# Weight splits moved from POOL to DVE, matmul operands aligned, and a regrouped top-k end, in a two-block kernel on one Trainium2 core

## The chip, the cores and the metric

The kernel runs on one core of one Trainium2 chip. A core has five engines that run side by side and wait for each other by semaphores: PE (TensorE, the matrix multiplier), DVE (VectorE), ACT (ScalarE), POOL (GpSimd) and SP (SyncE, which here only starts DMA transfers). On PE the profile also tells apart PEld, the loading of weights. The metric is the device time of one execution, in microseconds (us).

## The reference

The input is x, 256 tokens of 1,024 values, in fp32. The first block:

```python
proj = h @ w_in[l]                      # h = rmsnorm(x)
attn_out = windowed_gqa(q_a, k_a, v_a, attn_sink[l])
lru_out = bidir_rglru(centred_depthwise_conv(x_l, ...), ...) * gelu(gate_l)
mem_out = memory_cross_attention(q_m, k_m, v_m)
merged = (g[:, :, 0] * (attn_out @ p_attn[l]) + g[:, :, 1] * (lru_out @ p_lru[l])
          + g[:, :, 2] * (mem_out @ p_mem[l]))
x = x + merged @ w_out[l]
x = x + peer_ffn(rmsnorm(x, g_ffn[l]), w_peer_q[l], peer_sub_keys[l], peer_u[l], peer_v[l])
```

Its feed-forward picks experts by product keys:

```python
q = (h @ w_q).reshape(b, s, PEER_HEADS, 2, PEER_HALF)       # 8 heads, 2 halves of 128
sc = jnp.einsum('bshpc,hpkc->bshpk', q, sub_keys)           # 128 keys a half
top_v, top_i = lax.top_k(sc, PEER_TOPK)                     # 16 of each half
best_v, best_pos = lax.top_k(cand_v, PEER_TOPK)             # 16 of the 256 sums
gate = jax.nn.softmax(best_v, axis=-1)
act = jax.nn.gelu(jnp.einsum('chkd,cd->chk', u_tab[idx], hx))
out = jnp.einsum('chk,chkd->cd', gate * act, v_tab[idx])    # 16,384 experts in all
```

The second block has two hybrid layers. Each computes four branches from one projection (retention, a gated depthwise convolution of 31 taps, a gMLP, and sliding-window attention of 8 heads), projects and gates them, adds their sum through `w_out`, and ends with a SwiGLU feed-forward of width 2,816.

## The kernel before

**Layout and weights.** Features lie on the 128 partitions, the 256 tokens along the free axis. All weights are cut into blocks of 128 x 128, 5,416 in all, stored in HBM in the order of use. Class `Stream` brings them: SP loads 16 blocks (1 MB) into a `raw` tile (two buffers), and for every slot of 8 blocks `_slot` makes two tiles of the reduced format fp32r: ACT copies `raw` to `whi` (L88), then DVE or POOL forms `wlo = raw - whi` (L91). This pair of instructions is called a split here. `pool_share = (m, d)` tells how many of d slots go to POOL: one in two as a rule, and all of them from the second part of the top-k to the end of that phase. `on_pool`, `on_vector` and `on_scalar` remember the last such instruction of an engine, and `issue_after` places an instruction behind it.

**Matmuls.** Every block costs three matmuls of 256 columns (`mm3`, L171 to L173): `whi` by the operand's high part, `whi` by its low part, `wlo` by its high part. The operand (128 x 256, high and low) is the moving one; in some projections (`mm3a`, L177 to L179) the weights move instead. `group`, `proj_a` and `proj_b` run these over the blocks of a projection.

**Tiles of operands.** In block 1 `T8`, `T6` and `T4` are helpers that take tiles of 8, 6 and 4 rows of 256 tokens from the pool "b1"; in a hybrid layer `T4` takes them from "m{l}", where small tiles are opened ahead of them. The trace calls all of these `t`. `hh` and `hl` are the normed input in two parts, `ga` the weighted expert activations, `fh` and `fl` the operand of the feed-forward's output projection.

**Order of the work.** The program is written as a main stream of blocks with background tasks beside it. `add` registers a generator as a task; each pair of weight blocks calls `tick`, which steps every task whose count has run out, and the number it yields is the number of ticks (times `unit`) to its next step. A list scheduler then sets the final order on each engine. Slots have raised priority.

**The expert feed-forward.** The scores of all experts are computed densely. A u-block is 8 weight blocks (24 matmuls into `pu`); its gelu goes to `ha` (L759). While the top-k runs as a task (`picks`), the main stream does u-blocks by `u_while`; `early` is their number by the end of that phase. The task takes 4 head pairs times 2 token halves: `unit` computes scores `sc` (L937), top 16 of each half (`top16`, from MAX8 at L1047), the 256 sums and the picks by one-hot products `oh` (L975 to L980), and yields `TK_PACE` ticks:

```python
                    yield TK_PACE
                    if hq == 3:
                        gates(t)
                        yield 2
                        turn(t)
```

`gates` is the softmax: DVE forms `ge` (L987), ACT its exponential (L988). `turn` transposes the picks of a half on PE into `ptk` (L241). Then `build` makes the gate matrix by one-hot products on PE (`pgb`), L846 multiplies `ha` by `hb` for the u-blocks done early, four blocks an instruction, and the V loop makes `ga` (L184, L185) and adds up the output in `acc`, with the remaining u-blocks in between.

**The mixers of a hybrid layer.** The main stream projects; beside it tasks run the convolution (taps on DVE, `t<-up,hw,t`, L1121), the attention scores (L1218 to L1233) and retention (L1264, L1267). L919 adds a projection's output to x, L295 forms the next operand's low part.

Of the kernel before, what the change touches and what calls it, by code (L numbers as in the profile page):

```python
# [7 lines left out]
F32 = mybir.dt.float32  # L8
# [11 lines left out]
P = 128  # L20
S = 256
KD = 8
# [3 lines left out]
RAW_BUFS = 2  # L26
SLOT_BUFS = 3
N_HA = 96
HALF = 64
TK_PACE = 20  # L30
T_OH = 8
# [21 lines left out]
class Stream:  # L53
# [3 lines left out]
    def __init__(self, K, pool, w):  # L57
        self.K, self.pool, self.w = K, pool, w
        self.order = []
        self.ticked = 0  # L60
        self.raw = None
        self.cur = None
        self.pool_share = (1, 2)

# [63 lines left out]
class Core:  # L128
# [111 lines left out]
    def transpose(self, out, in_):  # L240
        self.nc.tensor.transpose(out, in_, self.ident)  # L241

    def scr(self, name):
        return self.tp.tile([P, S], F32, tag="scr", name=name, bufs=N_SCR)
# [165 lines left out]
    def block1(self):  # L410
        tc, nc, a, ws = self.tc, self.nc, self.a, self.ws
        with ExitStack() as st:
            p = st.enter_context(tc.tile_pool(name="b1", bufs=1))

            def T8(dt=F32R):
                return p.tile([P, KD, S], dt, tag="t8", name="t8", bufs=2)

            def T6(dt=F32, w=S):
                return p.tile([P, 6, w], dt, tag="t6", name="t6", bufs=8)

            def T4(dt=F32):
                return p.tile([P, 4, S], dt, tag="t4", name="t4", bufs=5)

# [16 lines left out]


            xl = T6(w=S + 3)
            nc.gpsimd.memset(xl[:, :, 0:2], 0.0)
            nc.gpsimd.memset(xl[:, :, S + 2:S + 3], 0.0)
# [289 lines left out]
    def peer(self):  # L734
# [4 lines left out]
        tc, nc, a, ws = self.tc, self.nc, self.a, self.ws  # L739
        with ExitStack() as st:  # L740
            p = st.enter_context(tc.tile_pool(name="pe", bufs=1))
# [29 lines left out]
            with tc.tile_pool(name="peg", bufs=1) as gp:  # L771
# [106 lines left out]
                assert ahead == NBLK  # L878
                ws.pool_share = (1, 2)
                tl = self.tp.tile([P, LAST, 2, S], F32R, tag="ld", name="tail", bufs=1)  # L880
# [42 lines left out]
    def topk(self, tp, i1, i2, gt, iot):  # L923
        nc, a, ws = self.nc, self.a, self.ws
# [87 lines left out]
        def picks():  # L1012
            with self.tc.issue_after(ws.on_pool):
                nc.gpsimd.tensor_copy(io, self.cst[:, None, C_IO:C_IO + 16].to_broadcast([P, 32, 16]))
            for hq in range(4):
                for t in range(2):
                    while hq not in qts:
                        yield 1
                    unit(hq, t, qts[hq])
                    if hq == t == 1:  # L1020
                        with self.tc.issue_after(ws.on_pool):
                            nc.gpsimd.tensor_copy(iot, self.cst[:, C_IO:C_IO + P, None].to_broadcast([P, P, 2]))
                    yield TK_PACE
                    if hq == 3:
                        gates(t)
                        yield 2
                        turn(t)
            yield 4
# [25 lines left out]
    def mixers(self, l):  # L1054
        tc, nc, a, ws = self.tc, self.nc, self.a, self.ws
        with ExitStack() as st:
            p = st.enter_context(tc.tile_pool(name=f"m{l}", bufs=1))
            par = p.tile([P, P2_COLS], F32, tag="par2", name="par2")
# [6 lines left out]
            def T4(dt=F32):  # L1065
                return p.tile([P, 4, S], dt, tag="t4", name="t4", bufs=13)

# [367 lines left out]
    def ffn(self, l):  # L1435
        tc, nc, a, ws = self.tc, self.nc, self.a, self.ws
        with ExitStack() as st:
            p = st.enter_context(tc.tile_pool(name=f"f{l}", bufs=1))
            fh = p.tile([P, FF, S], F32R, tag="fh", name="fh")
            fl = p.tile([P, FF, S], F32R, tag="fl", name="fl")  # L1440
# [168 lines left out]
```

## Time and profile before

| | |
|---|---|
| median of 3 runs | 2208.46 us (2206.96 to 2214.88) |
| profiled execution | 2205.13 us, span 2203.3 us |
| mean granted clock of TensorE | 0.971 of full speed |
| busiest engines | PE 94%, DVE 79%, ACT 53%, POOL 33% of the span |
| splits `wlo` | 430 on DVE, mean 1268 ns; 247 on POOL, mean 2501 ns |
| moved by DMA | 370.03 MB, mean 168 GB/s |

The stages in time: block 1's mixers to about 345 us, the top-k of the experts from there to about 500, the rest of the experts to about 1170, the first layer's mixers to about 1540, its feed-forward to about 1690, the second layer's mixers to about 2045, and its feed-forward to the end. A row of the trace gives a start or a group's count, a duration, the engine, the line, the operation, and "out<-in" tiles by name with shape; in square brackets stands how long the engine was idle before it and which instruction released it. PEclk is the clock granted to TensorE as a share of full speed (1.00 is 2.4 GHz, 0.50 is 1.2).

### The profile page before, as it was taken

What the parts mean: (1) busy time and instruction counts of PE and PEld (TensorE: products, weight loads), DVE (VectorE), ACT (ScalarE), POOL (GpSimd) and SP (SyncE); (2) the same over time, 40 slices, a digit from 0 to 9 for tenths busy, and PEclk for the clock granted to TensorE, in tenths of its full rate; (3) what the DMA queues carried; (4) which work ended last, traced back from release to release, by engine and by line L of the source; (5) the groups of instructions that cost most, each with busy time, mean ns of one, the idle gap of its engine ahead of it and who ended that gap; (6) DMA issues with size and microseconds to landing.
All of it is one profiled execution on the core that took longest, in us unless ns stands there. A gap on an engine that the chain in (4) does not pass through costs nothing. (4 is left out here: it accounts for less than half of the span.)

```text
span 2203.3 us, 41676 instructions
## 1 busy us (share of the span) xinstructions
PE 2067.6 (94%) x16818; PEld 2002.5 (91%) x16818; DVE 1741.0 (79%) x3117; ACT 1159.6 (53%) x1906; POOL 734.2 (33%) x361
## 2 busy tenths in 40 slices
PE   8879999959998999999998899999999889999999
PEld 7868999959998999999998778999999778999997
DVE  8837668998999888975557999976764999976772
ACT  5648654435554555545445555466555545465543
POOL 4424746830000000000003434654444434654443
PEclk9989999979999999999999999999999999999999
DMA  5343555424553444455554533454555533445554
GB/s 194 122 126 118 189 183 181 172 84 167 179 181 138 173 173 173 173 177 194 197 188 145 190 125 143 173 183 176 197 192 193 191 131 135 168 177 175 192 192 159
DMA packets 56925, 370.03 MB, mean 168 GB/s; under 512 B 6491, under 2 KB 10140, under 8 KB 13468
## 3 DMA queue, kind: packets, MB, share of 16 engines
q1 hardware_dynamic: 50256, 357.06, 45.5%
q10 hardware_dynamic: 6476, 10.31, 1.8%
q8 instruction: 131, 2.15, 0.4%
q14 instruction: 62, 0.51, 0.1%
HBM read 364.73 MB, written 2.62 MB: 167 GB/s over the span
## 5 line engine op out<-in xcount | busy, mean ns | idle before, releaser
L88 ACT ACTIVATE whi<-raw 128x1024 fp32r<-128x1024 f32 x677 | 716.5, 1060 | 731.0 <-PE acc L172 165.9
L91 POOL TENSOR_TENSOR wlo<-raw,whi 128x1024 fp32r<-128x1024 f32 x247 | 617.5, 2501 | 1324.6 <-ACT whi L88 1238.6
L91 DVE TENSOR_TENSOR wlo<-raw,whi 128x1024 fp32r<-128x1024 f32 x430 | 545.2, 1268 | 211.7 <-ACT whi L88 209.9
L171 PE MATMUL pu<-hh,whi 128*128 128x256 f32 x1024 | 291.0, 284 | 21.9 <-ACT whi L88 21.9
L173 PE MATMUL mm<-hh,wlo 128*128 128x256 f32 x1008 | 285.7, 284 | 7.3 <-DVE wlo L91 5.0
L173 PE MATMUL pu<-hh,wlo 128*128 128x256 f32 x1024 | 286.5, 280 | 0.0
L172 PE MATMUL pu<-hl,whi 128*128 128x256 f32 x1024 | 286.4, 280 | 0.0
L172 PE MATMUL mm<-hl,whi 128*128 128x256 f32 x1008 | 285.2, 283 | 0.0
L171 PE MATMUL mm<-hh,whi 128*128 128x256 f32 x1008 | 284.7, 282 | 0.0
L172 PE MATMUL acc<-ga,whi 128*128 128x256 f32 x1000 | 269.8, 279 | 5.1 <-DVE ga L185 5.1
L173 PE MATMUL acc<-ga,wlo 128*128 128x256 f32 x1000 | 269.2, 279 | 0.0
L171 PE MATMUL acc<-ga,whi 128*128 128x256 f32 x1000 | 249.3, 281 | 4.9 <-ACT ga L184 4.9
L1121 DVE SCALAR_TENSOR_TENSOR t<-up,hw,t 128x256 f32<-128x256 f32 x240 | 215.3, 901 | 3.7
L171 PEld LDWEIGHTS pu<-hh,whi 128*128 128x128 f32 x1024 | 195.3, 191 | 22.3 <-ACT whi L88 22.3
L173 PE MATMUL pg<-hh,wlo 128*128 128x256 f32 x704 | 198.9, 283 | 9.4 <-POOL wlo L91 6.3
L173 PEld LDWEIGHTS mm<-hh,wlo 128*128 128x128 f32 x1008 | 193.1, 192 | 11.2 <-DVE wlo L91 6.2
L171 PE MATMUL pg<-hh,whi 128*128 128x256 f32 x704 | 198.5, 282 | 1.2 <-ACT whi L88 1.2
L172 PE MATMUL pg<-hl,whi 128*128 128x256 f32 x704 | 197.4, 280 | 0.0
L172 PEld LDWEIGHTS mm<-hl,whi 128*128 128x128 f32 x1008 | 193.5, 192 | 2.9 <-issue 2.7
L171 PEld LDWEIGHTS mm<-hh,whi 128*128 128x128 f32 x1008 | 193.1, 192 | 1.5 <-issue 0.8
L172 PEld LDWEIGHTS pu<-hl,whi 128*128 128x128 f32 x1024 | 194.4, 190 | 0.0
L173 PEld LDWEIGHTS pu<-hh,wlo 128*128 128x128 f32 x1024 | 194.3, 190 | 0.0
(410 smaller groups left out, 5209.5 us busy)
## 6 DMA issues: line engine op xcount, KB each, us to landing
raw<-in_w SPq DMA_DIRECT2D x336, 1024.0 KB, 4.8
raw<-in_w SPq DMA_DIRECT2D x5, 512.0 KB, 5.5
bias<-bias_scr ACTq DMA_DIRECT2D x4, 512.0 KB, 6.8
bias_scr<-sbb ACTq DMA_DIRECT2D x4, 384.0 KB
cl<-in_cstl ACTq DMA_DIRECT2D x2, 576.0 KB, 3.7
x<-in_xT SPq DMA_DIRECT2D x4, 256.0 KB, 6.5
memt<-in_memT ACTq DMA_DIRECT2D x1, 1024.0 KB, 4.9
keys<-in_keysT ACTq DMA_DIRECT2D x1, 1024.0 KB
```

The costliest lines, as they stand in the source:

```text
L88: self.on_scalar = nc.scalar.activation(out=hi, in_=src, func=AF.Copy).ins
L91: i = eng.tensor_tensor(out=lo, in0=src, in1=hi.bitcast(F32), op=ALU.subtract)
L171: mm(out, lhsT=wh, rhs=xh, start=start, stop=False)
L172: mm(out, lhsT=wh, rhs=xl, start=False, stop=False)
L173: mm(out, lhsT=wl, rhs=xh, start=False, stop=stop)
L1121: nc.vector.scalar_tensor_tensor(out=cy[:, j, :], in0=up[:, j, i:i + S], scalar=hw[:, j * NT + i:j * NT + i + 1], in1=cy[:, j, :], op0=ALU ...
```

## The change

Three things are changed.

*Splits.* The rule of `pool_share` is (0, 1) from the start, so no slot goes to POOL, but for the top-k, where all slots still go to it. The assignment at the V loop's end goes. POOL's splits fall from 247 to 48, DVE's rise from 430 to 629. `io` is filled behind the last DVE split instead of the last POOL split.

*Places.* The operand tiles of block 1 and of the mixers get pools of their own, opened behind a small pad tile of 512 bytes; `f{l}` gets a pad too; `xl` becomes a tile of its own. In the new layout all moving operands that are not weights start at byte 704 of a KiB, but for the V loop's `tail`. In the old one `hh`, `hl`, `ga` and the operand of the last output stage did; `fh`, `fl` stood at 192, the mixers' `T4` tiles at 352, block 1's `T8` and `T4` at 736 and its `T6` at 192 to 864.

*The top-k's end.* `TK_PACE` goes from 20 to 22 ticks. The softmax of both token halves follows the last unit and `TK_LAST` = 20 more ticks, and both transposes six ticks later.

```diff
-TK_PACE = 20
+PAD = 128
+TK_PACE = 22
+TK_LAST = 20
-        self.pool_share = (1, 2)
+        self.pool_share = (0, 1)
+    def pad(self, pool):
+
+        self.nc.vector.memset(pool.tile([P, PAD], F32, tag="pad", name="pad"), 0.0)
     def block1(self):
+            pa = st.enter_context(tc.tile_pool(name="b1a", bufs=1))
+            self.pad(pa)
             p = st.enter_context(tc.tile_pool(name="b1", bufs=1))
 
             def T8(dt=F32R):
-                return p.tile([P, KD, S], dt, tag="t8", name="t8", bufs=2)
+                return pa.tile([P, KD, S], dt, tag="t8", name="t8", bufs=2)
...
-            xl = T6(w=S + 3)
+            xl = p.tile([P, 6, S + 3], F32, tag="xl", name="xl")
...
-                ws.pool_share = (1, 2)
                 tl = self.tp.tile([P, LAST, 2, S], F32R, tag="ld", name="tail", bufs=1)
...
         def picks():
-            with self.tc.issue_after(ws.on_pool):
+            with self.tc.issue_after(ws.on_vector):
...
                     yield TK_PACE
-                    if hq == 3:
-                        gates(t)
-                        yield 2
-                        turn(t)
+
+            yield TK_LAST
+            for t in range(2):
+                gates(t)
+            yield 6
+            for t in range(2):
+                turn(t)
             yield 4
...
     def mixers(self, l):
+            pa = st.enter_context(tc.tile_pool(name=f"a{l}", bufs=1))
+            self.pad(pa)
             p = st.enter_context(tc.tile_pool(name=f"m{l}", bufs=1))
...
-                return p.tile([P, 4, S], dt, tag="t4", name="t4", bufs=13)
+                return pa.tile([P, 4, S], dt, tag="t4", name="t4", bufs=13)
...
             p = st.enter_context(tc.tile_pool(name=f"f{l}", bufs=1))
+            self.pad(p)
```

The order of the instructions on an engine shows what moves. The first place is DVE at the end of the top-k. `oh` and `sl` are the one-hot picks of a unit, `e` and `gt` belong to the gate matrix and the transposed picks, `tv<-sc` opens the next unit. Before:

```order
L980 TENSOR_REDUCE sl_3807<-oh 128x32
L975 TENSOR_TENSOR oh<-ijf,io 128x512
L978 TENSOR_TENSOR oh<-oh,tf 128x512
L980 TENSOR_REDUCE sl_3809<-oh 128x32
L793 TENSOR_TENSOR e<-iot,i_3795 128x512 x2
L791 TENSOR_TENSOR e<-iot,i_3796 128x1024 x2
L1004 TENSOR_TENSOR gt<-ptk,gt 128x128
L1047 MAX tv<-sc 128x8
```

And in the changed program, on the same engine at the same unit:

```order
L988 TENSOR_REDUCE sl_3813<-oh 128x32
L983 TENSOR_TENSOR oh<-ijf,io 128x512
L986 TENSOR_TENSOR oh<-oh,tf 128x512
L988 TENSOR_REDUCE sl_3815<-oh 128x32
L1058 MAX tv<-sc 128x8
L1059 MAX_INDEX ti<-tv,sc 128x8
```

The last unit now follows the one before it directly; `e` and `gt` of the first half stood between them.

The second place is ACT around the first exponential of the softmax, with the copies of slots (`whi`) and the gelu of u-blocks (`ha<-pu`). Before:

```order
L88 ACTIVATE whi_5289<-raw_5287 128x1024
L759 ACTIVATE ha_3801<-pu_5129 128x256
L88 ACTIVATE whi_5319<-raw_5287 128x1024
L759 ACTIVATE ha_3801<-pu_5224 128x256
L988 ACT_TABLE_LOAD
L988 ACTIVATE ge_5349<-ge_5349 128x128
L88 ACTIVATE whi_5358<-raw_5356 128x1024
```

And in the changed program:

```order
L90 ACTIVATE whi_5387<-raw_5355 128x1024
L768 ACTIVATE ha_3807<-pu_5227 128x256
L90 ACTIVATE whi_5419<-raw_5417 128x1024
L768 ACTIVATE ha_3807<-pu_5324 128x256
L996 ACT_TABLE_LOAD
L996 ACTIVATE ge_5854<-ge_5854 128x128
L90 ACTIVATE whi_5449<-raw_5417 128x1024
```

Ahead of this exponential stand 20 copies of u-blocks before and 23 now; the second exponential stands behind 26 and 29.

The third place is DVE in the first layer's mixers, among the taps. Before:

```order
L91 TENSOR_TENSOR wlo<-raw,whi 128x1024
L1121 SCALAR_TENSOR_TENSOR t_14802<-up,hw,t_14802 128x256 x4
L1218 SCALAR_TENSOR_TENSOR t_15243<-pss,bias 128x2x128 x2
L1264 TENSOR_TENSOR w_15303<-t_14993,cl 64x512 x2
L1223 TENSOR_REDUCE sm<-t_15243 128x4
L1267 TENSOR_TENSOR t_14993<-t_14993,cl 128x512
L1224 TENSOR_TENSOR sm<-sm,sk 128x4
L91 TENSOR_TENSOR wlo<-raw,whi 128x1024
```

And in the changed program:

```order
L93 TENSOR_TENSOR wlo<-raw,whi 128x1024
L1134 SCALAR_TENSOR_TENSOR t_14800<-up,hw,t_14800 128x256 x2
L93 TENSOR_TENSOR wlo<-raw,whi 128x1024
L1134 SCALAR_TENSOR_TENSOR t_14800<-up,hw,t_14800 128x256 x2
L93 TENSOR_TENSOR wlo<-raw,whi 128x1024
L1134 SCALAR_TENSOR_TENSOR t_14800<-up,hw,t_14800 128x256 x2
L1231 SCALAR_TENSOR_TENSOR t_15241<-pss,bias 128x2x128 x2
L1277 TENSOR_TENSOR w_15301<-t_14991,cl 64x512 x2
```

A split stood after every few taps; now there are about twice as many on this engine, and taps and splits take turns.

## Rows read from the trace of the kernel before

**Rows 1.** The head and the first part of the page: the span, and busy time, share of the span and instructions of each engine.

```profile
span 2203.3 us, 41676 instructions
...
PE 2067.6 (94%) x16818; PEld 2002.5 (91%) x16818; DVE 1741.0 (79%) x3117; ACT 1159.6 (53%) x1906; POOL 734.2 (33%) x361
```

**Rows 2.** The view by windows. The columns are the stretch (us from the span's start), its length, the busy time and instructions of PE, PEld, DVE, ACT and POOL, the granted clock of TensorE, the share of DMA, and GB/s.

```profile
0.00:200.00 200.00, 163.76 (x1139) 149.45 (x1140) 140.30 (x291) 122.84 (x228) 79.50 (x48) 0.90 0.45 143
345.00:440.00 95.00, 94.33 (x800) 94.33 (x800) 92.30 (x294) 43.64 (x61) 76.12 (x34) 0.98 0.50 178
440.00:505.00 65.00, 36.83 (x279) 35.85 (x278) 62.84 (x242) 21.30 (x34) 24.00 (x11) 0.76 0.27 98
505.00:700.00 195.00, 194.62 (x1818) 193.30 (x1816) 177.30 (x380) 104.57 (x193) 0.00 (x0) 1.00 0.49 174
1175.00:1400.00 225.00, 202.00 (x1434) 186.62 (x1433) 210.65 (x335) 119.44 (x209) 94.51 (x46) 0.94 0.43 150
1550.00:1700.00 150.00, 150.00 (x1326) 150.00 (x1325) 93.69 (x84) 74.82 (x105) 66.89 (x28) 1.00 0.55 197
1700.00:1900.00 200.00, 180.56 (x1276) 164.57 (x1274) 185.27 (x287) 104.08 (x176) 84.11 (x41) 0.96 0.44 153
```

**Rows 3.** Groups of instructions by line, DVE from 1175 to 1400: line, engine, operation, tiles and shapes, count, then busy time and mean ns of one, then the idle time before them and what ended it.

```profile
L1121 DVE SCALAR_TENSOR_TENSOR t<-up,hw,t 128x256 f32<-128x256 f32 x100 | 85.3, 858 | 1.4
L91 DVE TENSOR_TENSOR wlo<-raw,whi 128x1024 fp32r<-128x1024 f32 x29 | 38.4, 1323 | 2.9 <-ACT whi L88 2.8
...
L919 DVE SCALAR_TENSOR_TENSOR x<-x,par,rb 128x256 f32<-128x256 f32 x8 | 7.5, 1008 | 0.0
L295 DVE SCALAR_TENSOR_TENSOR raw<-x,gg,raw 128x256 fp32r<-128x256 f32 x8 | 7.3, 930 | 0.0
```

**Rows 4.** The same view for the splits on POOL, first from 1175 to 1400, then from 1700 to 1900, then in the first 200 us.

```profile
L91 POOL TENSOR_TENSOR wlo<-raw,whi 128x1024 fp32r<-128x1024 f32 x30 | 76.8, 2560 | 106.2 <-ACT whi L88 83.1 <-DVE t L1121 9.6 <-PE mm L179 9.3
...
L91 POOL TENSOR_TENSOR wlo<-raw,whi 128x1024 fp32r<-128x1024 f32 x26 | 66.5, 2557 | 91.7 <-ACT whi L88 80.8 <-PE pp L173 4.3 <-PE pg L173 3.9
...
L91 POOL TENSOR_TENSOR wlo<-raw,whi 128x1024 fp32r<-128x1024 f32 x21 | 59.5, 2832 | 84.8 <-ACT whi L88 62.2 <-DVE t L185 7.8 <-PE mm L173 7.0
```

**Rows 5.** The same view, DVE from 1700 to 1900.

```profile
L1121 DVE SCALAR_TENSOR_TENSOR t<-up,hw,t 128x256 f32<-128x256 f32 x96 | 80.2, 840 | 1.3
L91 DVE TENSOR_TENSOR wlo<-raw,whi 128x1024 fp32r<-128x1024 f32 x26 | 37.5, 1444 | 2.2 <-ACT whi L88 2.1
```

**Rows 6.** The timeline of 1262 to 1276, DVE and POOL: start, duration, engine, line, operation, tiles, and how many alike stand in the row.

```profile
1262.64 0.48 DVE L1121 SCALAR_TENSOR_TENSOR t<-up,hw,t 128x256 f32<-128x256 f32 x1
...
1265.19 2.64 DVE L1121 SCALAR_TENSOR_TENSOR t<-up,hw,t 128x256 f32<-128x256 f32 x1
1265.21 2.34 POOL L91 TENSOR_TENSOR wlo<-raw,whi 128x1024 fp32r<-128x1024 f32 x1
...
1268.56 1.22 DVE L91 TENSOR_TENSOR wlo<-raw,whi 128x1024 fp32r<-128x1024 f32 x1
1269.70 1.67 DVE L1121 SCALAR_TENSOR_TENSOR t<-up,hw,t 128x256 f32<-128x256 f32 x4
```

**Rows 7.** The timeline of the top-k's end, in square brackets the idle time of the engine before the instruction and what ended it.

```profile
354.17 0.30 DVE L1047 MAX8 tv<-sc 128x8 f32<-128x128 f32 x1 [0.32 <-PE sc L937]
...
469.45 0.28 DVE L987 TENSOR_TENSOR ge<-bv 128x128 f32<-128x128 f32 x1
469.76 0.31 ACT L988 ACTIVATE ge<-ge 128x128 f32<-128x128 f32 x1 [24.27 <-DVE ge L987]
471.06 0.58 PE L171 MATMUL pu<-hh,whi 128*128 128x256 f32 x1 [19.72 <-ACT whi L88]
...
476.83 0.47 PE L241 MATMUL ptk<-cst,sl 128*128 128x128 f32 x1 [4.97 <-DVE sl L980]
...
500.54 0.48 PE L241 MATMUL ptk<-cst,sl 128*128 128x128 f32 x1 [2.69 <-DVE sl L980]
```

**Rows 8.** The multiplies of `ha` by `hb` by tile (count, then ns of the shortest, median and longest, and first and last start), and the timeline of PE behind them.

```profile
L846 DVE TENSOR_TENSOR ha<-ha,hb x9: 419/1220/1223, 704.3 to 713.1; 128x1024 f32<-128x1024 f32 x7, 128x768 f32<-128x768 f32 x1, 128x256 f32<-128x256 f32 x1
L846 DVE TENSOR_TENSOR ha<-ha x1: 422/422/422, 703.9 to 703.9; 128x256 f32<-128x256 f32 x1
...
713.88 0.39 PE L172 MATMUL acc<-ga,whi 128*128 128x256 f32 x1 [3.76 <-DVE ga L185]
```

**Rows 9.** Matmuls of one line by tile, in four stretches of the view by tile: count, then the shortest, median and longest duration in ns, and first and last start. A line has one of the three matmuls of a step; of `hh` two shapes share a row.

```profile
L171 PE MATMUL mm<-fh,whi x176: 276/276/276, 1632.2 to 1691.7; 128*128 128x256 f32 x176
...
L171 PE MATMUL mml<-t,whi x32: 279/284/286, 1485.8 to 1497.0; 128*128 128x256 f32 x32
...
L171 PE MATMUL mml<-t,whi x32: 277/280/285, 307.7 to 318.7; 128*128 128x256 f32 x32
...
L171 PE MATMUL mm<-hh,whi x272: 276/276/281, 2044.2 to 2138.0; 128*128 128x256 f32 x136
...
L171 PE MATMUL mm<-hh,whi x272: 276/276/276, 1539.7 to 1631.8; 128*128 128x256 f32 x136
```

**Rows 10.** The timeline of PE from 738 to 744, in the V loop.

```profile
738.79 0.28 PE L171 MATMUL acc<-ga,whi 128*128 128x256 f32 x1
...
739.58 0.28 PE L172 MATMUL acc<-ga,whi 128*128 128x256 f32 x1
...
740.83 0.63 PE L804 MATMUL pgb<-e1g,e 128*128 128x128 f16 x8
...
742.53 0.28 PE L172 MATMUL acc<-ga,whi 128*128 128x256 f32 x1
...
743.24 0.28 PE L172 MATMUL acc<-ga,whi 128*128 128x256 f32 x1
```

More of the change, by code (lines that the diff above doesn't have):

```diff
@@ L412, in block1, with T6 @@
         with ExitStack() as st:
+            pa = st.enter_context(tc.tile_pool(name="b1a", bufs=1))
+            self.pad(pa)
             p = st.enter_context(tc.tile_pool(name="b1", bufs=1))
             def T8(dt=F32R):
-                return p.tile([P, KD, S], dt, tag="t8", name="t8", bufs=2)
-            def T6(dt=F32, w=S):
-                return p.tile([P, 6, w], dt, tag="t6", name="t6", bufs=8)
+                return pa.tile([P, KD, S], dt, tag="t8", name="t8", bufs=2)
+            def T6(dt=F32):
+                return pa.tile([P, 6, S], dt, tag="t6", name="t6", bufs=8)
             def T4(dt=F32):
-                return p.tile([P, 4, S], dt, tag="t4", name="t4", bufs=5)
+                return pa.tile([P, 4, S], dt, tag="t4", name="t4", bufs=5)
             def raw16():
```

## The prediction

> **What bounds the kernel now.** First the page: PE is busy 94% of the span and DVE 79%, POOL a third [rows 1]. So the end is set by PE wherever it runs without gaps, and any gain must come from its gaps, its pace, or its clock. The view by windows tells the stretches apart [rows 2]. From 505 to 700 and 1550 to 1700 PE is full at granted clock 1.00, with DVE at 91% and 62%: there only the pace counts. From 1175 to 1400 and 1700 to 1900, the two mixer stages, PE is busy 90% and DVE 94% and 93%; here DVE sets the pace. From 440 to 505 PE is busy 37 of 65 us at clock 0.76 while DVE is at 97%: the end of the top-k. In the first 200 us no engine is full (DVE 140), so DVE is not the bound throughout there.
>
> **The splits moved to DVE.** POOL does 247 of the 677 splits `wlo = raw - whi`, DVE 430. After the change POOL keeps 48, all of the top-k, so 199 go to DVE. In the mixers 30 move in 1175 to 1400 and 26 in 1700 to 1900 [rows 4]. On DVE one follows the next instruction at 1.14 us (1268.56 to 1269.70), so they add 30 x 1.14 = 34.2 and 26 x 1.14 = 29.6 us of DVE time, nothing removed yet.
>
> Against that stands what POOL costs DVE. The timeline shows the same convolution tap taking 0.48 us at 1262.64 and 2.64 at 1265.19, which lies on POOL's split of 1265.21 for 2.34; without POOL four taps take 1.67, 0.418 each [rows 6]. Over the stage 100 taps take 85.3 us, mean 858 [rows 3]; at 0.418 they take 41.8, so 43.5 is time in which DVE stood. Of the two other two-input operations L919 gives 8 x (1008 - 480) = 4.2 and L295 8 x (930 - 480) = 3.6, taking 480 from the free tap. DVE's own 29 splits give 29 x (1323 - 1220) = 3.0, with the 1.22 of 1268.56 as the free one [rows 6]. Sum 54.3. POOL's splits are 76.8 [rows 4] of its 94.5 busy us [rows 2]; the rest of POOL stays and goes on blocking, so I take 0.81 of it: 44.0. Net 44.0 - 34.2 = 9.8 of DVE time. DVE is busy 210.65 of 225, so 9.8/0.936 = 10.5 us of the stage. In the second mixers 96 taps take 80.2 against 40.1, 26 own splits 26 x (1444 - 1220) = 5.8 [rows 5]; 45.9 x 66.5/84.1 = 36.3, less 29.6 is 6.7, over 0.926 is 7.2. That makes 17.7 as the lower end. If all the blocking ends with the splits, the same sums without the 0.81 and 0.79 give 20 + 16 = 36, over 0.93 is 39. Between 17.7 and 39 I take 26, nearer the lower, since it is not shown which of POOL's work blocks.
>
> In block 1 21 splits move in the first 200 us [rows 4], 21 x 1.14 = 24 added to 140.3 of 200, against a relief of the same kind; PE waits there for other things. I take 0, between 4 lost and 4 won. In the feed-forward stretches (1550 to 1700) at most the 28 instructions of POOL move and add 32 to 93.7 of 150 [rows 2]: PE's work hides them, and what it costs if that cover fails is a `wlo` that comes one DVE burst late. I take 0.
>
> The Trainium skill says of this, on its page "SBUF — State Buffer", section "Who interferes with whom", that a DVE instruction with two SBUF inputs contends with a GpSimd instruction that reads SBUF, and the loser waits out the whole operation. This trace agrees (2.64 on 2.34 [rows 6]).
>
> **The end of the top-k.** DVE runs almost without a pause (92.3 of 95 us, then 62.84 of 65 [rows 2]) from 354.17 to the subtraction `ge` at 469.45; then ACT, whose queue is in order, stands 24.27 us at the exponential behind it, and every `whi` copy is behind that. PE, its last operand used up, idles 19.72 [rows 7]. Two more stops follow, 4.97 and 2.69, where the transposes `ptk` wait for the sums of DVE. From 440 to 505 PE did 279 matmuls [rows 2]; at the pace of the stretch before (95 us over 800, 118.75 ns) they need 33.1, so 31.9 are lost: 19.72 + 4.97 + 2.69 and 4.5 of low clock (0.76). After the change the order of ACT has 23 copies of u-blocks ahead of the first exponential instead of 20: three more u-blocks of 24 matmuls at 118.75 ns are 8.5 us, and PE has work for so much longer, so its stop falls from 19.7 to about 11. Both exponentials now stand after the last unit, and the transposes six blocks' ticks behind them, so 4.97 and 2.69 go. 8.5 + 7.7, and 1 of the 4.5 of clock, is 17 in round numbers. What is late next is the same DVE chain, with the two units back to back and no transposes between them. Bounds: 5 if the exponential simply comes later as DVE gets the second unit ahead of it, and only the `ptk` waits shrink; 26 if nothing is left but 6 of the 31.9. I take 17. ACT still queues copies behind each exponential; that is why not more.
>
> **The batch multiplies of ha by hb** fall from 10 to 6 instructions of four blocks each, since more u-blocks are finished within the top-k. Before, nine of them took 704.3 to 713.1 with 1220 ns each, and PE then waited 3.76 for `ga` [rows 8]. Ten at 0.966 in sequence were 9.66 of DVE time, six are 6.3: 3.4 less in front of that wait. I take 3.4, between 0 (hidden) and 3.8.
>
> **The place of the moving operands.** In the layout of the program `hh` stands at byte 704 of a KiB and `fh` at 192, the mixers' `t` at 352, block 1's `t` of the row at 736; the change puts all of them at 704. 176 steps of three matmuls with `fh` start within 59.5 us: 59.5/(175 x 3) = 113.3 ns a matmul. The mixers' `t` needs 11.2/(31 x 3) = 120.4, block 1's 11.0/93 = 118.3, and the shortest durations are 279 and 277 beside 276 [rows 9]. By the program 240 blocks of each mixer layer have such a `t` as moving operand, three matmuls each, 1440 in all, and 296 blocks of block 1, 888: 1440 x 7.1 = 10.2 and 888 x 5.0 = 4.4. The slow pace also lasts: `hh` at 704 takes 93.8 us in the second feed-forward, right after such a stretch, and 92.1 for the same loop of the first [rows 9], 1.7 more. 16.3 in all. But `ga`, always at 704, goes from 113 ns (0.79 for 7 matmuls) to 118 (0.71 for 6) within one loop, across a group of one-hot products `pgb` [rows 10]: so the slow pace has another cause too, which the change leaves. Bounds: 23 won if the slow stretches that begin otherwise end too, and 7 lost if the new layout starts them earlier.
>
> The Trainium skill, page "TensorE: Matmul & The Clock Gate", section "Wait — 56ns, not 53.3ns?", gives the gap of back-to-back warm matmuls as the columns over 2.4 GHz and some 2.5 ns, whatever the address. By it this term is nothing. The rows have two paces for one shape, and the measurement decides as far as it reaches; the rival below keeps the rule's case.
>
> **Sum**, against the profiled execution of 2205.13: 26 (mixers) + 17 (top-k) + 3.4 (multiplies) + 16.3 (place) = 62.7, so 2142.4. The median of the runs shown, 2208.46, is 3.3 above the profiled one: 2146, rounded.
>
> **The rivals.** One: the place of the operands is worth nothing and the slow pace has another cause. For it speaks that it comes within a loop at one address [rows 10]; against it, that `t` is slow at each place where it stands elsewhere than 704 [rows 9]. Then 16.3 less: 2162. Two: the stop of the top-k only moves. DVE is full there [rows 2], and the exponential still needs the last unit's sums; what PE gains by the three u-blocks it loses since DVE comes as much later. 17 less: 2163. Three: in the mixers the relief is eaten by the new splits, which stand in DVE's order between the operations that release PE: 26 less, 2172. Two or three of these together give 2188 to 2205.
>
> Four, the other side: the slow taps are slow of themselves (their inputs, PSUM among them) and not by POOL's splits. Then nothing is given back, and 34.2 + 29.6 = 63.8 us stand on a DVE that is full at 93% in both mixers: 69 us of them, less the other 36, is 33 slower: 2241. For it: DVE's 94% [rows 2], so that each added split lies on the path. Against it: the 2.64 beside 0.48 in one place [rows 6]. It decides for slower than before once less than 30 of the 80 us of relief come back, and by over 0.5% once less than 20 do.
>
> **Chances.** Forecast 0.50 (its own range 2125 to 2165), rival one 0.16, two 0.13, three 0.07, several of them at once 0.06, rival four 0.08. A measurement of this kernel can tell about 0.5%, 11 us, from no change. Faster by more than that: 0.50 + 0.16 + 0.13 + 0.07 and half of the 0.06, 0.89; within it the other half, 0.03; slower 0.08. The range 2120 to 2185 leaves out rival four, half of the several at once and the lowest end of the forecast, under 2 in 10.
>
> **What would show it.** Mixers: taps of 0.42 to 0.5 us with no 2.6 among them, DVE still over 90% busy and the stage of 225 shorter by 10 to 20. Top-k: one idle stretch of PE of 9 to 13 us with ACT's exponential as its cause, and no wait for `ptk` over 1 us. Place: the mixers' `t` loops at 113 ns, with means of 276. Wrong would be: taps still at 850 on the mean, a stop of PE of 20 us or more at the exponential, the slow pace unchanged at 704, or new waits of PE for `wlo` from DVE in the feed-forward stretches.

## The result, and the profile after

The changed kernel takes 2123.62 us (median of 4 runs, 2122.92 to 2125.62), the kernel before 2210.15 beside it: ratio 0.961, 95% interval 0.959 to 0.963, so 86.5 us faster. Forecast were 2146 us, in a range of 2120 to 2185, and 62 us of gain. The direction and the stated range held, the range by 3.6 us; the forecast's own range, 2125 to 2165, was missed by 1.4. 24 us more than the forecast were won, and the sum was made of terms that err in both directions, so that the range held is in part luck.

The head and first part of the page of the changed kernel, beside [rows 1]:

```profile
span 2121.8 us, 41452 instructions
...
PE 2032.5 (96%) x16818; PEld 1974.2 (93%) x16818; DVE 1680.1 (79%) x3308; ACT 1164.8 (55%) x1910; POOL 252.3 (12%) x162
```

DVE has 199 splits more and is busy 60.9 us less, as if a split on POOL had cost DVE more time than doing it itself costs; the run below with the splits alone tests that. The splits on DVE fell from a mean of 1268 to 1238 ns.

To see where the time came from, both traces need marks that are the same work. ACT's copies `whi` are numbered alike in all of these kernels (677 of them, in the order of the weights), so the table gives the time from the start of one to the start of another; the first stretch is counted from the span's start, and the last to the end.

| stretch, by copies | before | changed | gain | forecast |
|---|---|---|---|---|
| block 1, 0 to 90 | 339.5 | 327.3 | 12.2 | 4.4 |
| top-k, 90 to 150 | 215.7 | 205.3 | 10.4 | 17 |
| experts, 150 to 355 | 612.9 | 613.8 | -0.9 | 3.4 |
| first layer's mixers, 355 to 470 | 390.8 | 362.1 | 28.7 | 36 for both mixers |
| second layer's mixers, 525 to 600 | 267.5 | 239.6 | 27.9 | (in the row above) |
| feed-forwards, 470 to 525 and 600 to the end | 377.0 | 373.6 | 3.4 | 1.7 |

**The mixers.** The view by windows, first of the kernel before over its two mixer stretches, then of the changed kernel over the same work (columns as in [rows 2]):

```profile
1168.10:1558.90 390.80, 363.34 (x2803) 346.96 (x2803) 338.12 (x497) 213.34 (x360) 183.57 (x91) 0.97 0.46 163
1709.50:1977.00 267.50, 245.71 (x1823) 229.07 (x1823) 246.87 (x358) 140.78 (x235) 128.09 (x67) 0.97 0.45 158
```
```profile
1146.50:1508.60 362.10, 349.97 (x2803) 334.66 (x2802) 311.23 (x555) 217.84 (x364) 40.93 (x33) 0.99 0.49 176
1659.20:1898.80 239.60, 233.49 (x1820) 220.67 (x1819) 221.16 (x398) 144.73 (x237) 35.44 (x29) 0.99 0.50 177
```

DVE, with 58 more instructions in the first stretch, is busy 26.9 us less (338.12 to 311.23), and 25.7 less in the second; the stretches become 28.7 and 27.9 shorter. The groups by line of DVE in the first stretch, before and after:

```profile
L1121 DVE SCALAR_TENSOR_TENSOR t<-up,hw,t 128x256 f32<-128x256 f32 x120 | 108.0, 904 | 1.8
L91 DVE TENSOR_TENSOR wlo<-raw,whi 128x1024 fp32r<-128x1024 f32 x58 | 75.6, 1303 | 12.8 <-ACT whi L88 12.1 <-PE pg L172 0.5
...
L185 DVE TENSOR_TENSOR fl<-fsg,fh 128x256 fp32r<-128x256 f32 x7 | 10.6, 1515 | 3.7 <-ACT fh L184 3.5
L257 DVE TENSOR_TENSOR nacc<-nacc,nsq 128x256 f32<-128x256 f32 x21 | 10.5, 516 | 0.1
```
```profile
L93 DVE TENSOR_TENSOR wlo<-raw,whi 128x1024 fp32r<-128x1024 f32 x115 | 142.3, 1237 | 33.6 <-ACT whi L90 33.2
L1134 DVE SCALAR_TENSOR_TENSOR t<-up,hw,t 128x256 f32<-128x256 f32 x120 | 62.8, 537 | 0.6
...
L263 DVE TENSOR_TENSOR nacc<-nacc,nsq 128x256 f32<-128x256 f32 x21 | 8.4, 420 | 0.0
```

The taps give 45.2 us back (108.0 to 62.8) and the splits take 66.7 (75.6 to 142.3). What balances this is spread over many small groups, of which `fl` and `nacc` are two. As a measure of the time in which DVE stood, take from each operation the duration that a tenth of its group (same line and tiles, whole trace) stay under, and add up the rest: 108.1 us before and 20.7 after in this stretch, 83.8 and 19.2 in the second. Of the taps in the first stretch 26 took over 1 us before, all of them while POOL was at work (23 beside a split), the longest 2.68; 3 do after, beside POOL's other work, the longest 1.52.

**The top-k's end.** The timeline of the changed kernel, to be read beside [rows 7]:

```profile
463.54 0.27 DVE L995 TENSOR_TENSOR ge<-bv 128x128 f32<-128x128 f32 x1
463.84 0.31 ACT L996 ACTIVATE ge<-ge 128x128 f32<-128x128 f32 x1 [24.87 <-DVE ge L995]
465.15 0.58 PE L173 MATMUL pu<-hh,whi 128*128 128x256 f32 x1 [20.27 <-ACT whi L90]
467.58 0.58 PE L175 MATMUL pu<-hh,wlo 128*128 128x256 f32 x1 [1.64 <-POOL wlo L93]
```

The stop of PE is as long as before, 20.27 for 19.72. PE has three more u-blocks ahead of it, 8.5 us by the forecast's pace, but DVE now does the top 16 and the sums of the last unit, 455.86 to 463.5, ahead of `ge`. The two waits for `ptk` are gone.

**The multiplies and the pace.** PE's wait for DVE's part of the first `ga` fell from 3.76 [rows 8] to 0.26:

```profile
L855 DVE TENSOR_TENSOR ha<-ha,hb x6: 1209/1210/1211, 708.1 to 713.8; 128x1024 f32<-128x1024 f32 x6
...
715.35 0.39 PE L174 MATMUL acc<-ga,whi 128*128 128x256 f32 x1 [0.26 <-DVE ga L187]
```

Not all of these 3.5 us are won. In both kernels PE does the same work between a group of one-hot products and this point. The group's row, before and after:

```profile
698.99 0.63 PE L804 MATMUL pgb<-e1g,e 128*128 128x128 f16 x8
...
703.06 0.63 PE L813 MATMUL pgb<-e1g,e 128*128 128x128 f16 x8
```

From it to the end of the wait are 14.89 us before (to 713.88) and 12.29 after: 2.6 us less, as the multiplies take 6.9 us (708.1 to 715.0) for 9.6. The rest of the wait is filled by matmuls that run longer at the lower clock: the granted clock is 0.51 from 709 to 714 here, and was 0.66 from 704 to 709 before.

The mixers' `t`, at byte 704 now, runs at the short duration, and 32 steps of three matmuls start within 10.6 us, not 11.2 [rows 9]:

```profile
L173 PE MATMUL mml<-t,whi x32: 276/276/276, 1439.4 to 1450.0; 128*128 128x256 f32 x32
```

But the slow pace has not gone: the excess over 113.3 ns from one 256-column matmul to the next adds up to some 34 us before and 26 after. In block 1 from 210 to 320 and in the V loop from 734 to 960 a matmul takes 117.8 ns, with every operand at 704.

### The profile page after: what moved, and what is told of

The parts are those of the page before. It is cut to its first block, busy times and chain, and to the rows that moved or that the text cites. A ratio compares the mean times of both kernels' runs of the same rounds, so it can differ in the third digit from the quotient of the medians.

```text
span 2121.8 us, 41452 instructions
## 1 busy us (share of the span) xinstructions
PE 2032.5 (96%) x16818; PEld 1974.2 (93%) x16818; DVE 1680.1 (79%) x3308; ACT 1164.8 (55%) x1910; POOL 252.3 (12%) x162
## 4 chain that ended last, share of the span: by engine, by line
PE 81%; DVE 9%; issue 3%; DMA 3%; ACT 3%; POOL 1%; ACTq 0%; SPq 0%; POOLq 0%; DVEq 0%
PE mm L175 6%; PE mm L173 6%; PE mm L174 6%; PE acc L174 5%; PE pu L173 5%; PE acc L175 5%; PE acc L173 5%; PE pu L175 5%; PE pu L174 5%; PE pg L175 3%; PE pg L174 3%; PE pg L173 3%; DVE wlo L93 2%; PE mml L173 2%; PE mml L175 2%
## 5 line engine op out<-in xcount | busy, mean ns | idle before, releaser
L93 DVE TENSOR_TENSOR wlo<-raw,whi 128x1024 fp32r<-128x1024 f32 x629 | 778.3, 1238 | 323.6 <-ACT whi L90 320.7
L175 PE MATMUL mm<-hh,wlo 128*128 128x256 f32 x1008 | 280.8, 279 | 5.3 <-DVE wlo L93 5.3
L174 PE MATMUL mm<-hl,whi 128*128 128x256 f32 x1008 | 280.3, 278 | 0.0
L174 PE MATMUL acc<-ga,whi 128*128 128x256 f32 x1000 | 267.9, 280 | 4.5 <-DVE ga L187 4.4
L173 PE MATMUL acc<-ga,whi 128*128 128x256 f32 x1000 | 242.5, 281 | 5.0 <-ACT ga L186 5.0
L174 PEld LDWEIGHTS acc<-ga,whi 128*128 128x128 f32 x1000 | 188.6, 189 | 5.3 <-DVE ga L187 5.3
L175 PEld LDWEIGHTS acc<-ga,wlo 128*128 128x128 f32 x1000 | 188.7, 189 | 0.0
```

The lines of the kernel that those rows point to most:

```text
L93: i = eng.tensor_tensor(out=lo, in0=src, in1=hi.bitcast(F32), op=ALU.subtract)
L173: mm(out, lhsT=wh, rhs=xh, start=start, stop=False)
L174: mm(out, lhsT=wh, rhs=xl, start=False, stop=False)
L175: mm(out, lhsT=wl, rhs=xh, start=False, stop=stop)
```

## The experiments

Theory (A in the expectations): POOL's splits held DVE up, and that made the mixers' gain; the place of operands gives some 14 us; the regrouping of the top-k little. Rivals: the places made it (B); the regrouping did.

**Each part alone or undone.** Four runs, beside the same repeats of the kernel before.

```diff
# e1: of the changed kernel, the rule of the splits undone
-        self.pool_share = (0, 1)
+        self.pool_share = (1, 2)
+                ws.pool_share = (1, 2)          # at the end of V
# e2: of the changed kernel, another pad
-PAD = 128
+PAD = 40
# e3: of the changed kernel, the old end of the top-k
-TK_PACE = 22
-TK_LAST = 20
+TK_PACE = 20
...
+                    if hq == 3:
+                        gates(t)
+                        yield 2
+                        turn(t)
# e4: of the kernel before, the rule of the splits alone
-        self.pool_share = (1, 2)
+        self.pool_share = (0, 1)
-                ws.pool_share = (1, 2)
-            with self.tc.issue_after(ws.on_pool):
+            with self.tc.issue_after(ws.on_vector):
```

> The changed kernel with every other split on POOL again (outside the top-k, as before); operand places and the top-k's end stay changed. Theory A, POOL's splits hold up DVE's two-input operations for their whole duration and this made the mixers' gain: slower than the changed kernel by 40 to 55 us, about 2170, taps back at a mean of 830 to 860 ns in the mixers, DVE's other operations there longer by some 40 us a layer. Theory B, the operand places made the mixers' gain: about 2130 to 2135, mixers at most 5 us a layer longer.

Measured 2195.72 us, ratio to before 0.995 (0.992 to 0.997): 72 us of the 86.5 gained are gone. The mixers are back at 390.1 and 266.4 us, the taps at 928 ns. Groups and windows of this run:

```profile
L1135 DVE SCALAR_TENSOR_TENSOR t<-up,hw,t 128x256 f32<-128x256 f32 x120 | 110.9, 928 | 1.8
```
```profile
1158.10:1548.20 390.10, 359.25 (x2803) 342.75 (x2802) 339.90 (x498) 212.78 (x359) 185.57 (x91) 0.97 0.47 163
```

With places and top-k changed and POOL's splits back, the first mixers have DVE's 339.9 and the length of before. That is theory A, and more of it than expected (40 to 55).

> The kernel before with the move of the splits to DVE alone (no change of places, old end of the top-k). Theory A (POOL's splits hold up DVE): 45 to 60 us faster than before, 2150 to 2165, taps at 0.5 us on the mean. Theory B (places made the gain): at most 15 us faster, 2195 or more, and DVE in the mixers still near 94%. If relief is given back only as forecast: 26 faster, about 2184.

Measured 2146.81, ratio 0.973 (0.970 to 0.977), 64 us faster, with the mixers at 362.8 and 244.4 and the taps as in the changed kernel:

```profile
L1120 DVE SCALAR_TENSOR_TENSOR t<-up,hw,t 128x256 f32<-128x256 f32 x120 | 62.8, 537 | 0.6
```
```profile
1158.40:1521.20 362.80, 350.98 (x2803) 337.27 (x2802) 312.04 (x555) 218.03 (x364) 42.85 (x33) 0.99 0.49 176
1671.80:1916.20 244.40, 235.46 (x1817) 221.82 (x1817) 221.85 (x397) 143.93 (x236) 34.20 (x29) 0.99 0.50 173
```

28.0 of the first mixers' 28.7 are here, with the old places, and 23.1 of 27.9 in the second; block 1 gains 11.5 of its 12.2. DVE is busy 1680.7 us in all, as in the changed kernel. The move of the splits is worth 64 to 72 us, the greater part of 86.5.

> The changed kernel with a pad of 40 floats instead of 128, so that all operand tiles of block 1, the mixers and the feed-forward's output stand at byte 352 of a KiB instead of 704; nothing else differs. If the place sets the pace (120 ns a matmul at 352, 113.3 at 704): about 3,000 matmuls by 7 ns, less what stands beside DVE's bound, 10 to 20 us slower, 2134 to 2144, with the mixers' t loops and fh at 118 to 120 ns. If the place is nothing: 2124 within 4 us, and t loops at 113.

Measured 2140.23, 16.6 slower than the changed kernel: the place counts. The view by tile, `fh` and `t` of this run, then of the changed kernel:

```profile
L175 PE MATMUL mm<-fh,wlo x157: 279/280/287, 1589.7 to 1645.9; 128*128 128x256 f32 x157
...
L173 PE MATMUL mm<-t,whi x32: 278/280/283, 1449.6 to 1460.8; 128*128 128x256 f32 x32
```
```profile
L175 PE MATMUL mm<-fh,wlo x153: 276/276/276, 1589.9 to 1641.6; 128*128 128x256 f32 x153
...
L173 PE MATMUL mm<-t,whi x32: 276/276/276, 1450.3 to 1460.8; 128*128 128x256 f32 x32
```

At 352 a step of three matmuls with `fh` takes 56.2/156 = 360 ns, 120 a matmul; at 704 it takes 51.7/152 = 340 ns, 113.4 a matmul. By stretches 3.1 and 3.4 us are lost in the mixers, 4.4 and 7.5 in the feed-forwards, where `hh` at 704 runs slow behind the stretch at 352, as in [rows 9]. Block 1 loses nothing against the changed kernel, which runs it at 117.8 ns from 210 to 320.

> The changed kernel with the old end of the top-k (softmax and transposes of each half behind its own last unit, pace 20). If regrouping is worth what was forecast (17 and 3.4 us): about 2144. If it only shifts PE's stop at the exponential and removes the two waits for the transposes, as the trace of the changed kernel suggests: 2128 to 2132, with one stop of about 20 us and two of 3 to 5. If it is worth nothing: 2124 within 3.

Measured 2133.23: the regrouping is worth 9.6 us, not 20. It lies in copies 90 to 150, 217.5 against 205.3 us. Three stops of PE stand where the changed kernel has the one of 20.27:

```profile
457.91 0.58 PE L172 MATMUL pu<-hh,whi 128*128 128x256 f32 x1 [23.05 <-ACT whi L89]
463.68 0.47 PE L242 MATMUL ptk<-cst,sl 128*128 128x128 f32 x1 [4.97 <-DVE sl L987]
...
489.56 0.33 PE L242 MATMUL ptk<-cst,sl 128*128 128x128 f32 x1 [1.99 <-DVE sl L987]
```

So in that stretch 7.0 us are the waits for `ptk`, and 2.8 a shorter stop at the exponential.

**Places, again.**

```diff
# e5: of the changed kernel, the pad's tile left out
     def pad(self, pool):
-        self.nc.vector.memset(pool.tile([P, PAD], F32, tag="pad", name="pad"), 0.0)
+        pass
# e11: of the kernel before, the new pools and the pad alone
```

> The changed kernel without the pad's memory, so that the operand tiles of the new pools stand at byte 192 of a KiB instead of 704; order of instructions as in the changed kernel but for the three memsets of the pad. If 192 and 704 are alike (half a KiB apart, as fh at 192 ran at 113.3 ns before): 2124 within 4 us. If only 704 is fast: up to 17 us slower, 2134 to 2141, as at 352. If place never mattered and the slow pace at 352 was chance: 2124 to 2140, with slow loops in other places than at 352.

Measured 2129.58 (2121.4 to 2141.95; ratio 0.958 to 0.971, overlapping that of the changed kernel). The time can't tell 4 us from 10, but the trace can: the mixers' `t` has a median of 276 ns in every group. So 192 is as good as 704 for the pace of `t`. The excess over 113.3 ns is some 25 us, for 26 at 704 and 41 at 352; that sum alone would prove little, for in e7 below it is about 40 with every operand at 704.

> The kernel before with the change of places alone. Forecast's term: 16 us faster, about 2194, with the mixers' t loops at 113. From the runs so far the old places cost 10 to 14 us with all the rest changed, and part of that is hidden here beside a DVE that is the bound of the mixers: 4 to 12 us faster, 2199 to 2207. If places are nothing: 2211 within 4.

Measured 2206.02, ratio 0.998 (0.9955 to 0.9996): 1 to 10 us faster, some 5 in the middle, the low end. The mixers' `t` has a median of 276 ns, but the mixers become only 2.4 and 1.4 shorter: with POOL's splits there DVE sets the pace, and the faster PE waits more, 29.2 us for 27.5 in the first mixers and 23.6 for 21.8 in the second. From e4 to e3, which differ by the places on kernels with the splits moved, it is 13.6.

**What holds the top-k's end.**

```diff
# e8: of the changed kernel
-            nc.scalar.activation(out=e, in_=e, func=AF.Exp)
+            with self.tc.issue_after(ws.on_scalar):
+                nc.scalar.activation(out=e, in_=e, func=AF.Exp)
# e7: of the changed kernel, no split on POOL at all
-            ws.pool_share = (1, 1)
-                        with self.tc.issue_after(ws.on_pool):
+                        with self.tc.issue_after(ws.on_vector):
                             nc.gpsimd.tensor_copy(iot, ...)
# e9: both
```

> The changed kernel with the softmax's exponentials placed on ACT behind the newest slot's copy at the point where the task issues them (34 u-blocks done instead of 24 and 30). If PE's stop of some 22 us at the end of the top-k comes from ACT standing at the exponential with copies queued behind it: the stop falls to under 5 us, 15 to 22 us faster than the changed kernel, 2102 to 2109. If DVE's chain of picks holds PE by another way (buffers, transposes, the first gate blocks): the stop comes back later, 2115 to 2124.

Measured 2125.02: nothing gained. ACT no longer waits at the exponential (both run late, from 494.84 on), and PE stops for as long at the next thing that needs the picks:

```profile
475.90 0.47 PE L243 MATMUL ptk<-cst,sl 128*128 128x128 f32 x1 [23.89 <-DVE sl L988]
```

So the exponential was only the first of those in line: DVE's chain of picks is what is late.

> The changed kernel with the 48 splits of the top-k on DVE as well, none on POOL at all. POOL's splits hold DVE's operations up there by some 64 us in the trace of the changed kernel, 48 splits at 1.14 us add 55 to a DVE that is full: theory A (blocked time is given back, as in the mixers) gives a top-k 5 to 10 us shorter, 2114 to 2120. Rival, the rows of the top-k are held up by less than that or the splits now stand behind long bursts of picks: 2124 to 2150, with PE waiting for wlo of DVE.

Measured 2107.84, ratio 0.953 (0.948 to 0.958), 16 us faster than the changed kernel, more than either expectation. Copies 90 to 150 take 180.5 us instead of 205.3, and PE has no stop of over 1.5 us there. A window of 65 us that holds both exponentials, and one of the pick operations, of the changed kernel first, then of this run:

```profile
425.00:490.00 65.00, 41.99 (x339) 41.27 (x338) 64.15 (x264) 23.29 (x34) 30.19 (x14) 0.82 0.29 99
...
L983 DVE TENSOR_TENSOR oh<-ijf,io x16: 678/686/2917, 354.7 to 489.5; 128x512 f16<-128x512 f16 x16
```
```profile
420.00:485.00 65.00, 65.00 (x555) 65.00 (x554) 63.61 (x238) 34.84 (x50) 0.00 (x0) 1.00 0.51 179
...
L983 DVE TENSOR_TENSOR oh<-ijf,io x14: 667/678/686, 356.8 to 472.1; 128x512 f16<-128x512 f16 x14
```

The picks took up to 2917 ns beside a POOL split and at most 686 without. By the measure used above DVE stood some 63 us in the changed kernel's top-k (327 to 490) and 4.4 here (329 to 480). Not all of the 24.8 us won there show in the time. In the profiled execution, which is the slowest of the four (2116.18; the others 2103.12 to 2109.38), the experts' stretch became 12.6 longer (626.4 for 613.8), some 5 of it in the u-blocks of copies 150 to 210, which run at 117.8 ns where they ran at 113.3.

> Both of the last two: all splits on DVE, and the exponentials late. If each is worth what theory A says, 2095 to 2105 and the fastest of all. If without POOL DVE has no time for the splits of the top-k, slower than with late exponentials alone by 10 or more, 2112 to 2140.

Measured 2106.60 (0.947 to 0.957): the same as e7 within its range. Late exponentials add nothing here either.

**The slow pace.** Where the pace turns, in seven of the traces so far, nearly always a group of other matmuls stands. A single 128-column fp32 `sc` product turned the fast pace slow in 15 of 15 cases and the slow one fast in 21 of 23. Counted over all twelve traces, wherever the pace is clear on both sides, the number in a row tells more: one or three of these products turned the pace in 98 of 99 cases, two or four left it as it was in 37 of 39.

```diff
# e10: of e7, in build
                         products(i, *cur)
                         yield PACE[c0]
+                        if i == (6 if c0 else 3):
+                            tg = self.bg.tile([P, 4, P], F32, tag="bg", name="tgl")
+                            nc.tensor.matmul(tg[:, 0, :], lhsT=self.ident, rhs=self.ident, start=True, stop=True)
+                            yield 2
```

> The kernel with all splits on DVE (the run without POOL in the top-k), and two single 128-column fp32 matmuls whose result nobody reads, one among the u-blocks after the fourth group of one-hot products, one early in the loop of V. In the traces so far PE has two steady paces at the same place 704, 113.3 and 117.8 ns, and a single 128-column fp32 matmul between steps turned the one into the other in 36 of 38 cases, while groups of eight one-hot products left the slow one slow. If such an interruption sets the pace: from each of the two on the pace falls from 117.8 to about 114, some 150 us of u-blocks and 220 us of V shorter by 3.4%, 10 to 13 us faster than without, 2095 to 2099. If the pace has another cause: 2108 within 4, at 117.8 throughout.

Measured 2101.51, ratio 0.950 (0.947 to 0.953). The median is 6 us under that of e7 and the lowest of all, but the interval overlaps those of e7 and e9. Around the first of the two added matmuls, which the profile shows as two records each:

```profile
506.31 0.28 PE L173 MATMUL pu<-hh,whi 128*128 128x256 f32 x1
...
507.49 0.28 PE L174 MATMUL pu<-hl,whi 128*128 128x256 f32 x1
507.61 0.28 PE L175 MATMUL pu<-hh,wlo 128*128 128x256 f32 x1
507.73 0.39 PE L846 MATMUL tgl<-cst 128*128 128x128 f32 x2
...
508.08 0.28 PE L174 MATMUL pu<-hl,whi 128*128 128x256 f32 x1
...
509.21 0.28 PE L175 MATMUL pu<-hh,wlo 128*128 128x256 f32 x1
```

Ten matmuls before it take 1.18 us (506.31 to 507.49), ten behind it 1.13 (508.08 to 509.21). It lasts: u-blocks from 560 to 640, of e7 and of this run:

```profile
L173 PE MATMUL pu<-hh,whi x208: 281/281/363, 559.9 to 640.0; 128*128 128x256 f32 x104
```
```profile
L173 PE MATMUL pu<-hh,whi x215: 276/276/365, 559.9 to 639.8; 128*128 128x256 f32 x108
```

The second, at 738.49 in the V loop, turned the pace too, but it held for 9 us only. Behind this group of one-hot products the pace was slow again, and stayed so until beyond 1010:

```profile
747.54 0.63 PE L813 MATMUL pgb<-e1g,e 128*128 128x128 f16 x8
```

The first half of the expectation held, the second did not; why such a group turns the pace back here, while among the u-blocks the fast pace outlasts them, was not tried.

That the 6 us come from the added matmuls is not shown. In the profiled executions the stretch of block 1, which ends ahead of both, differs by more: 320.2 us in e10 for 329.0 in e7, 5.6 of it in copies 40 to 90. From 210 to 320, e7 first, then e10:

```profile
210.00:320.00 110.00, 110.00 (x934) 109.93 (x933) 75.81 (x109) 71.37 (x104) 15.88 (x15) 1.00 0.56 198
210.00:320.00 110.00, 110.00 (x972) 110.00 (x972) 79.49 (x116) 72.85 (x108) 18.08 (x15) 1.00 0.56 204
```

The order of the instructions on PE, DVE and ACT is the same there, and so is the clock, yet one runs at 117.8 and the other at 113.3 ns. And the u-blocks of copies 150 to 210, 193.4 us in e7 and 186.6 in e10, take 187.9 in the changed kernel, which has no such matmul. What the traces do show is the turn itself at each of the two.

## Why the prediction was right, and where its steps were wrong

**Splits: the mechanism right, the term too small by more than half (26 for the mixers and 0 for block 1; 64 to 72 measured).** The step that failed is the size of the relief in the mixers: 26 us forecast, 28.0 and 23.1 measured with the splits alone. The prediction took 54.3 us of DVE's waiting in 1175 to 1400, from the taps, L919, L295 and DVE's own splits. By the measure above DVE stood 65.8 us there, since groups that the sum left out were held up as well, and 42.3 more up to 1559: with both mixers 94 POOL splits moved, and not 56. The factor for what POOL still does was right: of 108.1 us 87.4 came back, which is the 0.81 of the forecast, and of 83.8 in the second mixers 64.6, 0.77 for its 0.79. So was the cost, 66.7 us for 57 splits, 1.17 each for 1.14. The last step, net DVE time by its busy share, held within a tenth: by the shares of the whole stretches 26.9/0.865 is 31.1 for the 28.7 measured, and 25.7/0.923 is 27.8 for 27.9. In block 1 I took 0 because DVE was not full there. Yet its operations other than splits, their durations added up, went from 196.6 to 143.7 us while 44 splits came, and block 1 was 11.5 us shorter in the profiled execution of the splits alone: a share of busy time under 100% does not tell that DVE is off the path, and busy time itself held the waiting.

**Feed-forwards: right.** Their moved splits cost nothing; 150.6 us both times.

**Top-k: wrong by half.** "PE has work for so much longer, so its stop falls from 19.7 to about 11" did not hold: it was 20.27, which the prediction had named as a sign of being wrong. Rival two came for this step: PE's three u-blocks of 8.5 us were eaten by DVE doing 7.7 us of the last unit ahead of `ge`, in an order of DVE that was shown ahead of the prediction. The two `ptk` waits went, and e3 has 9.6 us in all, the multiplies among them. Why DVE is late was not in the prediction at all: the same splits of POOL that were reckoned with in the mixers stand in the top-k too, and there they stayed.

**Multiplies: right in kind, a little too large.** 3.4 forecast, 2.6 won. The sum had six instructions at 6.3 us, which does not follow from ten at 0.966 each; they took 6.9. In the length of the experts' stretch the gain does not show; the slow pace of the V loop stands beside it there.

**Places: right in size, 16.3 forecast; 13.6 by e3 and e4, 16.6 lost at 352, some 5 on the kernel before.** Rival one fell with that: the mixers' `t` has 120 ns a matmul at 352 in the kernel before, e4 and e2, and 113 to 114 at 704 or 192. From e4 to e3 the mixers become 7.7 us shorter, for 10.2 forecast. But block 1's share of 4.4 is not shown: with all at 704 it is at 117.8 ns from 210 to 320, and the 118.3 that the prediction put down to byte 736 lies beside that slow pace. The persistence and "another cause", which stood there as a doubt, are as large as the term. The Trainium skill ("TensorE: Matmul & The Clock Gate", "Wait — 56ns, not 53.3ns?") gives the gap of warm back-to-back matmuls from their columns alone, for 256 of them 109.2 ns (an estimate by its formula), and does not speak of places. The 113.3, 117.8 and 120 ns of one shape here, at full granted clock, don't agree with one gap for a shape, and the measurement decides.

Rival three fell with e4, and so did the slower one, rival four: with the splits alone moved the taps take 537 ns, so they were not slow of themselves. One sign did not come: DVE was to stay over 90% busy in the mixers, and it is at 86% in the first (311.23 of 362.10) and 92% in the second.

That the total lies in the stated range is luck in this much: the mixers and block 1 gave more than their terms, which made up for the top-k that gave less.

## What to carry to other kernels

Work handed to POOL is not free because POOL is idle: compare the durations of DVE's operations while POOL runs and while it doesn't, over all groups and not the largest alone, and ask what the same work would cost on DVE. Here, in the first mixers, a split of 1.17 us on DVE took the place of one that had cost DVE about 1.5 us of waiting (87 us over 57). When an engine stops at one instruction, look what else behind it waits for the same producer before you move that instruction: e8 moved the wait, e7 removed it.

## What was not expected of the hardware

At one place in memory PE has two steady paces for a 256-column matmul, 113.3 and 117.8 ns, and stays in either for up to hundreds of microseconds. One or three 128-column fp32 products in a row turned it in 98 of 99 cases in the traces, two or four in 2 of 39, and a single one both times in e10. Which pace a stretch begins with is not settled by the program's order: the same order in block 1 ran at either, which is most of 5.6 us over copies 40 to 90. So a difference of some 6 us between two kernels can be this pace and not the change, and has to be looked for in the stretch that the change touches. At byte 352 of a KiB a matmul is slower than either, 120 ns; 192 and 704 are alike. Those two are multiples of 64 bytes and 352 is not, but no run tests whether that is the rule. What sets the two paces inside the engine stays open, and so does how to hold the fast one through the V loop, where some 8 us remain (an estimate: 220 us at 117.8 for 113.3 ns).
